# Down projection: the sums and low parts of the Strassen groups on VectorE instead of VectorE and GpSimd in turns

## The chip, the cores and the metric

The kernel runs on one core of a Trainium2 chip. The metric is the device time of one execution in microseconds (us). TensorE does the matmuls, VectorE (DVE in the rows) and GpSimd (POOL) the elementwise sums, ScalarE (ACT) the roundings and activations, and SyncE (SP) issues the loads and stores of this part.

## The reference

A layer with gated token mixers (windowed attention and an SSD scan), a cross-attention and a squared-ReLU MLP, in fp32, for 1024 tokens of width 1024. The part that matters here is the last one, the down projection of the MLP, a product of (1024 x 4096) by (4096 x 1024), and the final norm:

```python
        h = rmsnorm(x, norm_ffn[i])
        x = x + jnp.square(jax.nn.relu(h @ w_up[i])) @ w_down[i]
    return rmsnorm(x, norm_final)
```

## The kernel before, in words

An fp32 product is done as three matmuls of a reduced format: each operand is split into a high part (ScalarE rounds it, line 1305) and a low part (operand minus high part, line 1306), and high x high, high x low and low x high are accumulated.

`down_phase` walks over the 4096 hidden rows. The first 512 and the last 512 rows of the product are done plainly (`mm3`, lines 81 to 86). The 3072 rows between are three groups of 1024, each an object of class `Pair`: one level of Strassen-Winograd, so a group is seven products of 512-size blocks instead of eight. A product is 48 matmuls (line 1427): 4 row tiles t, and for each 4 slices k of the inner dimension by 3 matmuls. I call the seven products of a group its steps 1 to 7; `Pair.ORDER` gives their Strassen numbers (1, 2, 6, 5, 7, 3, 4).

While TensorE does one step, the other engines prepare the next one. A step's preparation is `split(n)`: 8 half tiles of 128 x 512 (4 of the left operand, 4 of the right), each one rounded by ScalarE and then subtracted (the low part). Some operands are sums of blocks; `early`, `s2`, `t6`, `s4` and `t4` make them with `op` (line 1271), also 128 x 512 each, 32 for a group, in place in the loaded rows or in the tiles `xy`. After every row tile VectorE adds the bank of PSUM to the running result (`add`, line 1331), since GpSimd does not read PSUM here.

The split tiles `kt` have four buffers, two for a step, so the rounding for the step after next can only start when TensorE is done with the step before. Rows of the hidden activations (`d_u`) and of the weights (`in_wdn_dram`) come in by SyncE (`load`, line 1255) into buffers that are reused as soon as their last reader is done.

TensorE's order is the written one; the other engines' queues are ordered by a scheduler from the code's dependencies and the units that `deal` hands out between the row tiles.

Of the kernel before, what the change touches and what calls it, by code (L numbers as in the profile page):

```python
# [7 lines left out]
F32 = mybir.dt.float32  # L8
# [3 lines left out]
ALU = mybir.AluOpType  # L12
# [57 lines left out]
def wload(kx, src, n=1024, hi=None, lo=None, eng=None):  # L70
    if hi is None:
        hi = kx.wp.tile([P, 1024], F32R, tag="wop", bufs=6, name="whi")[:, :n]
        lo = kx.wp.tile([P, 1024], F32R, tag="wop", bufs=6, name="wlo")[:, :n]
    split_in(kx, src, hi, lo, eng)
    return hi, lo
# [508 lines left out]
def attn_phase(kx, ins, dr):  # L584
    nc, tc = kx.nc, kx.tc
    V, A, G, PE = nc.vector, nc.scalar, nc.gpsimd, nc.tensor
    with tc.tile_pool(name="p2", bufs=1) as ap:
# [31 lines left out]
        for kv in range(4):  # L619
# [63 lines left out]
            def values(qb, t4):  # L683
                kb0, kb1 = max(qb - 1, 0), min(qb + 2, NT)
                nb = kb1 - kb0
                pts = []
                for kb in range(nb):
                    pt = kx.pp.tile([P, 512], F32, tag="p", name="pt")
                    for i in range(4):
                        PE.transpose(pt[:, i * P:(i + 1) * P], t4[:, i, kb * P:(kb + 1) * P], kx.ident)  # L690
                    ph = ap.tile([P, 512], F32R, tag="ph", bufs=4, name="ph")
                    pl = ap.tile([P, 512], F32R, tag="pl", bufs=4, name="pl")
                    A.activation(ph, pt, AF.Copy)
                    V.tensor_tensor(pl, pt, ph.bitcast(F32), ALU.subtract)
                    pts.append((ph, pl))
                op = kx.pp.tile([P, 512], F32, tag="p", name="op")
                for kb in range(nb):
                    v2 = vhl[:, kb0 + kb, kv].rearrange("p s q -> p (s q)")
                    PE.matmul(op, v2, pts[kb][0], start=kb == 0, stop=False)
                    PE.matmul(op, v2, pts[kb][1], start=False, stop=kb == nb - 1)  # L700
                oa = ap.tile([64, 512], F32, tag="oa", bufs=2, name="oa")
                ob = ap.tile([64, 512], F32, tag="ob", bufs=1, name="ob")
                A.activation(oa, op[0:64], AF.Copy)
                A.activation(ob, op[64:128], AF.Copy)
                G.tensor_tensor(oa, oa, ob, ALU.add)
                half = kv % 2
                nc.sync.dma_start(dr.at[kv // 2][qb // 4][64 * half:64 * half + 64, :, (qb % 4) * P:(qb % 4) * P + P],
                                  oa.rearrange("p (i c) -> p i c", i=4))
# [10 lines left out]
def merge_cross_phase(kx, ins, dr, x1_open):  # L719
    nc, tc = kx.nc, kx.tc  # L720
    V, A, G, PE = nc.vector, nc.scalar, nc.gpsimd, nc.tensor
    with tc.tile_pool(name="p3", bufs=1) as mp:
# [52 lines left out]
        def load_wo(ch, eng):  # L775
            ts = []
            for k2 in range(4):
                raw = kx.wp.tile([P, 1024], F32, tag="raw", bufs=kx.raw_bufs, name="raw")
                nc.sync.dma_start(raw, ins["wo"][ch, k2])
                for j in range(2):  # L780
                    t = t4k("wo")
                    rj = raw[:, j * 512:(j + 1) * 512]
                    A.activation(t[:, 0], rj, AF.Copy)
                    eng.tensor_tensor(t[:, 1], rj, t[:, 0].bitcast(F32), ALU.subtract)
                    ts.append(t)
            return ts
# [80 lines left out]
        def values(hd, p2, ok):  # L867
            ph, pl = p2
            op = kx.pp.tile([P, 512], F32, tag="p", name="xop")
            for kb in range(2):  # L870
                vs = slice(kb * 512 + hd * P, kb * 512 + hd * P + P)
                ks = slice(kb * 512, (kb + 1) * 512)
                mm3(kx, op, (vxh[:, vs], vxl[:, vs]), (ph[:, ks], pl[:, ks]), kb == 0, kb == 1)
            A.activation(ok[:, hd, 0], op, AF.Copy)
            V.tensor_tensor(ok[:, hd, 1], op, ok[:, hd, 0].bitcast(F32), ALU.subtract)
# [124 lines left out]
def kt_tile(kx):  # L1000
    return kx.mp.tile([P, 4, 2, 512], F32R, tag="kt", bufs=4, name="kt")
# [25 lines left out]
def split_wd(kx, ins, hl, m, raw, eng):  # L1027
    nc = kx.nc
    if ins is not None:
        nc.sync.dma_start(raw, ins["wdn"][m])  # L1030
    nc.scalar.activation(hl[0], raw, AF.Copy)
    eng.tensor_tensor(hl[1], raw, hl[0].bitcast(F32), ALU.subtract)


class Up:
# [138 lines left out]
    def quad(self, b, stage, nxt):  # L1174
# [21 lines left out]
        else:  # L1196
# [8 lines left out]
            after()  # L1205
        c12 = self.t2("c12")
        product(pb, 6, early)
        whole(c12, pb)
        after()
# [30 lines left out]
class Pair:  # L1240
# [26 lines left out]
        k, h = (int(name[1]) - 1, int(name[2]) - 1) if name[0] == "b" else (int(name[2]) - 1, int(name[1]) - 1)  # L1267
        return t[4 * k + j][:, 512 * h:512 * h + 512]

    def op(self, eng, out, x, y, alu, j):  # L1270
        eng.tensor_tensor(self.half(out, j), self.half(x, j), self.half(y, j), alu)

    def early(self, j):

        V, G, op = self.kx.nc.vector, self.kx.nc.gpsimd, self.op
        pool = self.fp if j < 2 else self.kx.wp
        self.xy[j] = pool.tile([P, D], F32, tag="raw", bufs=2, name="xy")
        return [lambda: op(V, "x", "a11", "a21", ALU.subtract, j), lambda: op(G, "y", "b22", "b12", ALU.subtract, j),
                lambda: op(V, "a21", "a21", "a22", ALU.add, j), lambda: op(G, "b12", "b12", "b11", ALU.subtract, j)]

    def eng(self, j, odd):
        return self.kx.nc.gpsimd if j % 2 != odd else self.kx.nc.vector

    def s2(self, j):
        self.op(self.eng(j, 0), "a11", "a21", "a11", ALU.subtract, j)

    def t6(self, j):
        self.op(self.eng(j, 1), "b11", "b22", "b12", ALU.subtract, j)

    def s4(self, j):  # L1290
        self.op(self.eng(j, 0), "a12", "a12", "a11", ALU.subtract, j)

    def t4(self, j):
        self.op(self.eng(j, 1), "b21", "b21", "b11", ALU.subtract, j)

    def split(self, n):

        nc = self.kx.nc
        left, right = {1: ("a11", "b11"), 2: ("a12", "b21"), 6: ("a11", "b11"), 5: ("a21", "b12"), 7: ("x", "y"),
                       3: ("a12", "b22"), 4: ("a22", "b21")}[n]  # L1300
        self.lr = lt, rt = kt_tile(self.kx), kt_tile(self.kx)

        def step(t, name, eng, j):
            src = self.half(name, j)
            nc.scalar.activation(t[:, j, 0], src, AF.Copy)  # L1305
            eng.tensor_tensor(t[:, j, 1], src, t[:, j, 0].bitcast(F32), ALU.subtract)  # L1306

        return [lambda t=t, name=name, eng=eng, j=j: step(t, name, eng, j) for j in range(4)
                for t, name, eng in ((lt, left, nc.vector), (rt, right, nc.gpsimd))]


def down_phase(kx, ins, dr, first, out):
# [252 lines left out]
```

## Time and profile before

| what | us |
|---|---|
| median of 3 runs | 2473.14 (2465.56 to 2475.99) |
| the profiled execution | 2473.64 |
| its span | 2471.9 |
| TensorE busy in the span | 2371.6 |
| VectorE busy | 1456.7 |
| GpSimd busy | 1199.7 |
| ScalarE busy | 1107.9 |

The span is the time from the first to the last recorded instruction; what lies around it is 1.7 us. Busy times overlap. The down projection's groups lie between 2173.7 and 2420.5 us of the span.

### The profile page before, as it was taken

Reading aid. Unit: us, or ns where it says so; the run is one execution under the profiler, and the core shown is the slowest. Engines: PE = TensorE matmul, PEld = TensorE weight load, DVE = VectorE, ACT = ScalarE, POOL = GpSimd, SP = SyncE. Lnnn points to the kernel's source line nnn. Section 1 sums busy time; section 2 is a strip of 40 time slices with the busy share of each in tenths; the row PEclk is TensorE's granted clock in tenths of the full one; section 3 lists DMA queues with packets and bytes.
Section 4 is the critical chain, followed back from the end, with each engine's and each line's share of the span. In section 5 each row is a group of like instructions: output and inputs, shape, how many; then the busy total and the mean of one; then the engine's idle time right before and its main releaser. Section 6 shows DMA issues by size and latency. Waiting matters only on the chain.

```text
span 2471.9 us, 32466 instructions
## 1 busy us (share of the span) xinstructions
PE 2371.6 (96%) x12012; PEld 1965.7 (80%) x12012; DVE 1456.7 (59%) x2120; ACT 1107.9 (45%) x2310; POOL 1199.7 (49%) x1013
## 2 busy tenths in 40 slices
PE   7899999999999999999999999999998999999998
PEld 6687887878888787777777878888986887877777
DVE  5747566575765654465564242334676456689884
ACT  5436354463635545566774242224543333133332
POOL 4235436353452633344553444324486444488870
PEclk9999999999999999999999999999999999999999
DMA  6214223231322322111116363512243345712301
GB/s 227 78 60 128 60 94 102 68 121 56 116 69 86 112 65 80 50 41 56 43 52 221 128 213 128 204 43 77 91 164 116 109 134 175 285 68 85 111 26 69
DMA packets 154926, 260.46 MB, mean 105 GB/s; under 512 B 11792, under 2 KB 86672, under 8 KB 154768
## 3 DMA queue, kind: packets, MB, share of 16 engines
q1 hardware_dynamic: 83872, 219.58, 25.6%
q10 hardware_dynamic: 70896, 38.81, 5.5%
q8 instruction: 95, 1.56, 0.2%
q14 instruction: 63, 0.52, 0.1%
HBM read 210.90 MB, written 47.45 MB: 105 GB/s over the span
## 4 chain that ended last, share of the span: by engine, by line
PE 57%; DVE 13%; POOL 11%; ACT 8%; issue 6%; DMA 4%; ACTq 0%; POOLq 0%; SPq 0%; DVEq 0%
PE pb L1146 6%; PE dps L1427 5%; PE mps L86 3%; PE mps L85 3%; PE mps L81 3%; PE pc L1146 3%; PE zp L85 2%; PE zp L81 2%; PE zp L86 2%; POOL wlo L67 2%; PE st L462 2%; DVE cx L350 2%; POOL prev L477 2%; POOL kt L1306 1%; ACT whi L66 1%
## 5 line engine op out<-in xcount | busy, mean ns | idle before, releaser
L67 POOL TENSOR_TENSOR wlo<-raw,whi 128x1024 fp32r<-128x1024 f32 x142 | 350.1, 2467 | 596.2 <-ACT whi L66 556.7
L66 ACT ACTIVATE whi<-raw 128x1024 fp32r<-128x1024 f32 x144 | 152.0, 1055 | 254.6 <-PE mps L85 115.5
L1427 PE MATMUL dps<-kt 128*128 128x512 f32 x1008 | 234.1, 394 | 12.8 <-POOL kt L1306 12.7
L1427 PEld LDWEIGHTS dps<-kt 128*128 128x128 f32 x1008 | 190.8, 190 | 56.0 <-POOL kt L1306 16.2
L81 PE MATMUL cps<-kt,whi 128*128 128x512 f32 x512 | 217.5, 425 | 8.6 <-DVE cx L350 8.6
L86 PE MATMUL cps<-kt,wlo 128*128 128x512 f32 x512 | 201.5, 394 | 0.0
L85 PE MATMUL cps<-kt,whi 128*128 128x512 f32 x512 | 200.8, 392 | 0.0
L1305 ACT ACTIVATE kt<-row 128x512 fp32r<-128x512 f32 x144 | 77.2, 618 | 156.7 <-PE dps L1427 119.7
L1306 POOL TENSOR_TENSOR kt<-row,kt 128x512 fp32r<-128x512 f32 x72 | 117.5, 1653 | 22.8 <-ACT kt L1305 22.8
L1092 POOL TENSOR_TENSOR wop<-w,wop 128x512 fp32r<-128x512 f32 x64 | 86.1, 1347 | 84.8 <-ACT wop L1091 75.9
L81 PEld LDWEIGHTS cps<-kt,whi 128*128 128x128 f32 x512 | 97.3, 190 | 34.6 <-issue 16.0
L85 PEld LDWEIGHTS cps<-kt,whi 128*128 128x128 f32 x512 | 97.5, 190 | 26.2 <-issue 7.2
L86 PEld LDWEIGHTS cps<-kt,wlo 128*128 128x128 f32 x512 | 96.9, 189 | 20.9
L120 POOL TENSOR_TENSOR rr<-rv,mhalf 128x1 f32<-128x1 f32 (+1 forms) x50 | 38.6, 772 | 152.2 <-DVE rv L118 149.6
L680 POOL TENSOR_SCALAR t<-t,den 128x384 f32<-128x384 f32 (+1 forms) x128 | 69.1, 559 | 82.0 <-DVE den L678 65.9
L81 PE MATMUL gps<-kt,whi 128*128 128x512 f32 x256 | 108.8, 425 | 0.0
L496 ACT ACTIVATE ef<-rows,ebias 128x128 f32<-128x128 f32 x256 | 83.2, 390 | 53.3 <-PE cb L511 49.9
L86 PE MATMUL mps<-yk,wlo 128*128 128x512 f32 x256 | 100.9, 394 | 4.8 <-POOL wlo L67 4.8
L1146 PE MATMUL pb<-kt,wop 128*128 128x512 f32 x384 | 94.8, 396 | 9.5 <-ACT c L1200 9.1
L86 PE MATMUL gps<-kt,wlo 128*128 128x512 f32 x256 | 101.5, 396 | 0.0
L85 PE MATMUL mps<-yk,whi 128*128 128x512 f32 x256 | 100.7, 393 | 0.2 <-DVE yk L734 0.2
L85 PE MATMUL gps<-kt,whi 128*128 128x512 f32 x256 | 100.9, 394 | 0.0
(381 smaller groups left out, 6964.8 us busy)
## 6 DMA issues: line engine op xcount, KB each, us to landing
rows<-d_cs ACTq DMA_DIRECT2D x128, 256.0 KB, 3.7
raw<-in_wssd_dram SPq DMA_DIRECT2D x48, 512.0 KB, 3.3
raw<-in_wup_dram SPq DMA_DIRECT2D x40, 512.0 KB, 3.6
raw<-in_wsb_dram SPq DMA_DIRECT2D x32, 512.0 KB, 3.2
d_u<-c SPq DMA_DIRECT2D x64, 256.0 KB, 2.3
row<-in_wdn_dram SPq DMA_DIRECT2D x28, 512.0 KB, 6.3
row<-d_u SPq DMA_DIRECT2D x28, 512.0 KB, 7.0
x<-in_x_dram SPq DMA_DIRECT2D x16, 512.0 KB, 6.0
```

What stands on the lines that cost most here:

```text
L66: nc.scalar.activation(hi, raw, AF.Copy)
L67: (eng or nc.gpsimd).tensor_tensor(lo, raw, hi.bitcast(F32), ALU.subtract)
L81: i = mm(out, l[0], r[0], start=first, stop=False)
L85: mm(out, l[0], r[1], start=False, stop=False)
L86: mm(out, l[1], r[0], start=False, stop=last)
L496: A.activation(ef[:, h], rows[:, 0, h], AF.Exp, bias=kx.ebias[:, b, j, 0, o:o + 1])
L680: G.tensor_scalar(t4[:, i, :n], t4[:, i, :n], den[:, i:i + 1], 1.0, ALU.mult, ALU.mult)
L1092: self.kx.nc.gpsimd.tensor_tensor(t[:, 1], src, t[:, 0].bitcast(F32), ALU.subtract)
L1146: self.kx.nc.tensor.matmul(ps, w[:, i, ks], act[:, k, j], start=start and k == 0 and m == 0, stop=k == 3 and m == 2, skip_group_check=True)
L1305: nc.scalar.activation(t[:, j, 0], src, AF.Copy)
L1306: eng.tensor_tensor(t[:, j, 1], src, t[:, j, 0].bitcast(F32), ALU.subtract)
L1427: PE.matmul(ps[t], lt[:, k, x, ts], rt[:, k, y], start=n in (1, 2, 5) and k == 0 and m == 0, stop=k == 3 and m == 2, skip_group_check=True)
```

## The change

Every sum (`early`, `s2`, `t6`, `s4`, `t4`) and every low part of the groups (`split`) is issued on VectorE. Before, about half of them were on GpSimd: the right operands' low parts, the sums of the right operand in `early`, and by turns (`eng`) the others. Nothing is added or removed, and no load is moved in the code. The low parts of the last 512 weight rows (`split_wd`, line 1032) and a tiny power (line 120) stay on GpSimd.

```diff
-    def op(self, eng, out, x, y, alu, j):
-        eng.tensor_tensor(self.half(out, j), self.half(x, j), self.half(y, j), alu)
+    def op(self, out, x, y, alu, j):
+        self.kx.nc.vector.tensor_tensor(self.half(out, j), self.half(x, j), self.half(y, j), alu)
...
-        return [lambda: op(V, "x", "a11", "a21", ALU.subtract, j), lambda: op(G, "y", "b22", "b12", ALU.subtract, j),
-                lambda: op(V, "a21", "a21", "a22", ALU.add, j), lambda: op(G, "b12", "b12", "b11", ALU.subtract, j)]
-
-    def eng(self, j, odd):
-        return self.kx.nc.gpsimd if j % 2 != odd else self.kx.nc.vector
+        return [lambda: op("x", "a11", "a21", ALU.subtract, j), lambda: op("y", "b22", "b12", ALU.subtract, j),
+                lambda: op("a21", "a21", "a22", ALU.add, j), lambda: op("b12", "b12", "b11", ALU.subtract, j)]
 
     def s2(self, j):
-        self.op(self.eng(j, 0), "a11", "a21", "a11", ALU.subtract, j)
+        self.op("a11", "a21", "a11", ALU.subtract, j)
 
     def t6(self, j):
-        self.op(self.eng(j, 1), "b11", "b22", "b12", ALU.subtract, j)
+        self.op("b11", "b22", "b12", ALU.subtract, j)
...
-        def step(t, name, eng, j):
+        def step(t, name, j):
             src = self.half(name, j)
             nc.scalar.activation(t[:, j, 0], src, AF.Copy)
-            eng.tensor_tensor(t[:, j, 1], src, t[:, j, 0].bitcast(F32), ALU.subtract)
-
-        return [lambda t=t, name=name, eng=eng, j=j: step(t, name, eng, j) for j in range(4)
-                for t, name, eng in ((lt, left, nc.vector), (rt, right, nc.gpsimd))]
+            nc.vector.tensor_tensor(t[:, j, 1], src, t[:, j, 0].bitcast(F32), ALU.subtract)
+
+        return [lambda t=t, name=name, j=j: step(t, name, j) for j in range(4)
+                for t, name in ((lt, left), (rt, right))]
```

The first place is step 6 of the first group, where step 7's operands are split (tiles `kt_19463` left, `kt_19464` right) and the next group's rows (`row_19487`, `row_19489`, `row_19512`, `row_19514`) have just been asked for. VectorE's queue before:

```order
L1306 TENSOR_TENSOR kt_19463<-row_18768,kt_19463 128x512
L1306 TENSOR_TENSOR kt_19463<-row_18776,kt_19463 128x512
L1331 TENSOR_TENSOR xl_18756<-xl_18756,dps_19064 128x512
L1306 TENSOR_TENSOR kt_19463<-row_18784,kt_19463 128x512
L1306 TENSOR_TENSOR kt_19463<-row_18792,kt_19463 128x512
L1271 TENSOR_TENSOR row_19331<-row_19331,row_19487 128x512
L1331 TENSOR_TENSOR xl_18758<-xl_18758,dps_19065 128x512
L1271 TENSOR_TENSOR row_19353<-row_19353,row_19512 128x512
L1331 TENSOR_TENSOR xl_18760<-xl_18760,dps_19066 128x512
L1331 TENSOR_TENSOR xl_18762<-xl_18762,dps_19067 128x512
```

GpSimd's queue before, in the same step:

```order
L1306 TENSOR_TENSOR kt_19464<-row_18770,kt_19464 128x512
L1306 TENSOR_TENSOR kt_19464<-row_18778,kt_19464 128x512
L1306 TENSOR_TENSOR kt_19464<-row_18786,kt_19464 128x512
L1306 TENSOR_TENSOR kt_19464<-row_18794,kt_19464 128x512
L1271 TENSOR_TENSOR xy_19548<-row_19489,row_19333 128x512
L1271 TENSOR_TENSOR row_19333<-row_19333 128x512
L1271 TENSOR_TENSOR xy_19549<-row_19514,row_19355 128x512
L1271 TENSOR_TENSOR row_19355<-row_19355 128x512
```

VectorE's queue of the changed kernel from the step's seventh low part to its last add (lines shifted by 3):

```order
L1303 TENSOR_TENSOR kt_19463<-row_18792,kt_19463 128x512
L1328 TENSOR_TENSOR xl_18758<-xl_18758,dps_19065 128x512
L1303 TENSOR_TENSOR kt_19464<-row_18794,kt_19464 128x512
L1271 TENSOR_TENSOR xy_19548<-row_19489,row_19333 128x512
L1271 TENSOR_TENSOR row_19331<-row_19331,row_19487 128x512
L1271 TENSOR_TENSOR row_19333<-row_19333 128x512
L1328 TENSOR_TENSOR xl_18760<-xl_18760,dps_19066 128x512
L1271 TENSOR_TENSOR row_19353<-row_19353,row_19512 128x512
L1271 TENSOR_TENSOR xy_19549<-row_19514,row_19355 128x512
L1271 TENSOR_TENSOR row_19355<-row_19355 128x512
L1328 TENSOR_TENSOR xl_18762<-xl_18762,dps_19067 128x512
```

The step's 18 instructions stand in one queue: eight low parts with two adds between them, then the sums that wait for the newly loaded rows, with the last two adds behind those.

The second place is the beginning of the phase, where the plain part's adds (tiles `dps`, line 1331 before) give banks of PSUM back. VectorE before:

```order
L1331 TENSOR_TENSOR xl_18760<-xl_18760,dps_18852 128x512
L1331 TENSOR_TENSOR xl_18760<-xl_18760,dps_18866 128x512
L1271 TENSOR_TENSOR row_18772<-row_18772,row_18776 128x512
L1331 TENSOR_TENSOR xl_18762<-xl_18762,dps_18880 128x512
L1271 TENSOR_TENSOR xy_18918<-row_18780 128x512
L1331 TENSOR_TENSOR xl_18762<-xl_18762,dps_18894 128x512
```

The same stretch of VectorE's queue in the changed kernel:

```order
L1328 TENSOR_TENSOR xl_18760<-xl_18760,dps_18852 128x512
L1328 TENSOR_TENSOR xl_18760<-xl_18760,dps_18866 128x512
L1271 TENSOR_TENSOR xy_18917<-row_18778,row_18774 128x512
L1271 TENSOR_TENSOR row_18774<-row_18774 128x512
L1271 TENSOR_TENSOR row_18772<-row_18772,row_18776 128x512
L1328 TENSOR_TENSOR xl_18762<-xl_18762,dps_18880 128x512
L1271 TENSOR_TENSOR xy_18918<-row_18780 128x512
L1271 TENSOR_TENSOR xy_18918<-row_18786,row_18782 128x512
L1328 TENSOR_TENSOR xl_18762<-xl_18762,dps_18894 128x512
```

Three sums of weight rows (`row_18774`, `row_18778`, `row_18782`, `row_18786`) now stand ahead of the last two adds.

## Rows read from the trace of the kernel before

**Rows 1.** Busy time of each engine in the stretch of the groups: stretch, its length, and for each engine busy us and instructions; then TensorE's granted clock as a share of 2.4 GHz, and the share and rate of the DMA engines.

```profile
2173.70:2420.47 246.77, 233.96 (x1009) 190.94 (x1009) 219.84 (x214) 93.66 (x172) 196.68 (x120) 0.99 0.20 73
```

**Rows 2.** TensorE's instructions in order of time, from the plain part's first matmul to the last part's first one: start, length of the run, instruction and count; in brackets how long the engine sat idle before it and whom it waited for.

```profile
2130.18 0.39 PE L81 MATMUL dps<-kt 128*128 128x512 f32 x1
...
2173.72 46.42 PE L1427 MATMUL dps<-kt 128*128 128x512 f32 x202
2221.50 32.95 PE L1427 MATMUL dps<-kt 128*128 128x512 f32 x144 [1.36 <-POOL kt L1306]
2256.21 11.18 PE L1427 MATMUL dps<-kt 128*128 128x512 f32 x48 [1.76 <-POOL kt L1306]
2269.64 34.56 PE L1427 MATMUL dps<-kt 128*128 128x512 f32 x144 [2.25 <-POOL kt L1306]
2305.57 32.95 PE L1427 MATMUL dps<-kt 128*128 128x512 f32 x144 [1.36 <-POOL kt L1306]
2340.11 10.49 PE L1427 MATMUL dps<-kt 128*128 128x512 f32 x45 [1.59 <-POOL kt L1306]
2352.63 0.98 PE L1427 MATMUL dps<-kt 128*128 128x512 f32 x3 [2.03 <-POOL kt L1306]
2355.98 64.65 PE L1427 MATMUL dps<-kt 128*128 128x512 f32 x278 [2.38 <-POOL kt L1306]
2420.47 0.39 PE L81 MATMUL dps<-wd,kt 128*128 128x512 f32 x1
```

**Rows 3.** The same columns as rows 1, in two short stretches right behind one of those waits.

```profile
2269.64:2271.64 2.00, 2.00 (x6) 1.58 (x7) 2.00 (x3) 0.00 (x0) 2.00 (x2) 0.61 0.00 0
2271.64:2273.64 2.00, 2.00 (x7) 1.59 (x6) 2.00 (x4) 0.00 (x0) 2.00 (x2) 0.54 0.00 0
```

**Rows 4.** VectorE and GpSimd in order of time ahead of one of those waits (first VectorE, then GpSimd).

```profile
2250.31 3.48 DVE L1271 TENSOR_TENSOR row<-row 128x512 f32<-128x512 f32 x2
2253.71 0.67 DVE L1331 TENSOR_TENSOR x<-x,dps 128x512 f32<-128x512 f32 x1
...
2249.80 1.74 POOL L1271 TENSOR_TENSOR row<-row 128x512 f32<-128x512 f32 x1
2251.49 1.75 POOL L1306 TENSOR_TENSOR kt<-row,kt 128x512 fp32r<-128x512 f32 x1
...
2254.89 1.26 POOL L1306 TENSOR_TENSOR kt<-row,kt 128x512 fp32r<-128x512 f32 x1
```

**Rows 5.** VectorE in order of time at three places where GpSimd ran nothing: low parts of the last part's rows (line 1024), sums, and adds out of PSUM; the last row is GpSimd where VectorE ran nothing.

```profile
2410.46 2.50 DVE L1024 TENSOR_TENSOR kt<-row,kt 128x512 fp32r<-128x512 f32 x4
2161.78 1.28 DVE L1271 TENSOR_TENSOR row<-row 128x512 f32<-128x512 f32 x2
2172.90 4.86 DVE L1331 TENSOR_TENSOR x<-x,dps 128x512 f32<-128x512 f32 x8
2164.44 2.55 POOL L1306 TENSOR_TENSOR kt<-row,kt 128x512 fp32r<-128x512 f32 x2
```

**Rows 6.** Instructions by line and shape in the groups' stretch: count, busy us and mean ns of one, then idle time before them and what ended it.

```profile
L1306 DVE TENSOR_TENSOR kt<-row,kt 128x512 fp32r<-128x512 f32 x68 | 88.4, 1327 | 1.6 <-ACT kt L1305 1.6
L1271 DVE TENSOR_TENSOR row<-row 128x512 f32<-128x512 f32 x28 | 45.3, 1632 | 5.4 <-POOL kt L1306 4.2 <-DMA row<-d_u 1.0
L1331 DVE TENSOR_TENSOR xl<-xl,dps 128x512 f32<-128x512 f32 x48 | 31.8, 677 | 11.8 <-PE dps L1427 11.8
L1331 DVE TENSOR_TENSOR x<-x,dps 128x512 f32<-128x512 f32 x42 | 27.1, 676 | 2.4 <-PE dps L1427 2.4
L1306 DVE TENSOR_TENSOR kt<-xy,kt 128x512 fp32r<-128x512 f32 x12 | 16.9, 1437 | 4.0 <-ACT kt L1305 4.0
L1271 DVE TENSOR_TENSOR xy<-row 128x512 f32<-128x512 f32 x8 | 14.0, 1773 | 0.0
...
L1306 POOL TENSOR_TENSOR kt<-row,kt 128x512 fp32r<-128x512 f32 x68 | 111.9, 1667 | 22.8 <-ACT kt L1305 22.8
L1271 POOL TENSOR_TENSOR row<-row 128x512 f32<-128x512 f32 x28 | 44.3, 1582 | 3.0 <-DVE kt L1306 1.9
L1306 POOL TENSOR_TENSOR kt<-xy,kt 128x512 fp32r<-128x512 f32 x12 | 19.8, 1663 | 8.9 <-ACT kt L1305 4.5 <-DMA row<-in_wdn_dram 4.5
L1271 POOL TENSOR_TENSOR xy<-row 128x512 f32<-128x512 f32 x8 | 12.5, 1562 | 0.8 <-issue 0.3 <-DMA row<-in_wdn_dram 0.2
L1032 POOL TENSOR_TENSOR wd<-row,wd 128x1024 fp32r<-128x1024 f32 x4 | 10.0, 2509 | 2.0 <-ACT wd L1031 2.0
```

**Rows 7.** ScalarE's roundings around step 6 of the first group, in order of time.

```profile
2230.46 4.28 ACT L1305 ACTIVATE kt<-row 128x512 fp32r<-128x512 f32 x8 [8.28 <-PE dps L1427]
```

**Rows 8.** SyncE's first issue of a load in that step, of eight; the loads of the last stretch of the program by source, with size and median time from issue to landing; and the longest piece of a load in the chain that ended last: start and length.

```profile
2231.93 0.32 SPq L1255 DMA_DIRECT2D row<-d_u  x1
...
row<-in_wdn_dram SPq DMA_DIRECT2D x28, 512.0 KB, 6.3
row<-d_u SPq DMA_DIRECT2D x28, 512.0 KB, 7.0
...
2204.97 7.92 DMA row<-in_wdn_dram
```

**Rows 9.** GpSimd in order of time at the phase's beginning, where its sums wait for loads of weight rows.

```profile
2148.26 1.29 POOL L1271 TENSOR_TENSOR xy<-row 128x512 f32<-128x512 f32 x1 [7.86 <-DMA row<-in_wdn_dram]
2152.01 1.30 POOL L1271 TENSOR_TENSOR xy<-row 128x512 f32<-128x512 f32 x1 [0.65 <-DMA row<-in_wdn_dram]
```

More of the change, by code (lines that the diff above doesn't have):

```diff
@@ L1268, in half @@
         return t[4 * k + j][:, 512 * h:512 * h + 512]
-    def op(self, eng, out, x, y, alu, j):
-        eng.tensor_tensor(self.half(out, j), self.half(x, j), self.half(y, j), alu)
+    def op(self, out, x, y, alu, j):
+        self.kx.nc.vector.tensor_tensor(self.half(out, j), self.half(x, j), self.half(y, j), alu)
     def early(self, j):
-        V, G, op = self.kx.nc.vector, self.kx.nc.gpsimd, self.op
+        op = self.op
         pool = self.fp if j < 2 else self.kx.wp
         self.xy[j] = pool.tile([P, D], F32, tag="raw", bufs=2, name="xy")
-        return [lambda: op(V, "x", "a11", "a21", ALU.subtract, j), lambda: op(G, "y", "b22", "b12", ALU.subtract, j),
-                lambda: op(V, "a21", "a21", "a22", ALU.add, j), lambda: op(G, "b12", "b12", "b11", ALU.subtract, j)]
-    def eng(self, j, odd):
-        return self.kx.nc.gpsimd if j % 2 != odd else self.kx.nc.vector
+        return [lambda: op("x", "a11", "a21", ALU.subtract, j), lambda: op("y", "b22", "b12", ALU.subtract, j),
+                lambda: op("a21", "a21", "a22", ALU.add, j), lambda: op("b12", "b12", "b11", ALU.subtract, j)]
     def s2(self, j):
-        self.op(self.eng(j, 0), "a11", "a21", "a11", ALU.subtract, j)
+        self.op("a11", "a21", "a11", ALU.subtract, j)
     def t6(self, j):
-        self.op(self.eng(j, 1), "b11", "b22", "b12", ALU.subtract, j)
+        self.op("b11", "b22", "b12", ALU.subtract, j)
     def s4(self, j):
-        self.op(self.eng(j, 0), "a12", "a12", "a11", ALU.subtract, j)
+        self.op("a12", "a12", "a11", ALU.subtract, j)
     def t4(self, j):
-        self.op(self.eng(j, 1), "b21", "b21", "b11", ALU.subtract, j)
+        self.op("b21", "b21", "b11", ALU.subtract, j)
     def split(self, n):
```

## The prediction, made before the changed kernel was run

> **What bounds the kernel now.** I read the windows first. In the 246.77 us of the three groups TensorE is busy for nearly all, VectorE for 219.84 and GpSimd for 196.68 [rows 1]: three engines near their limit, so small differences between them show as waits. TensorE's own order in time says what is lost. From its first matmul of the groups at 2173.72 to the next part's first at 2420.47 are 246.75 us [rows 2]. The plain part before it, 192 matmuls without a wait, takes 2173.72 - 2130.18 = 43.54 us, 0.2268 us for one [rows 2]. The groups' 1008 matmuls would take 228.6 us at that pace. So 18.2 us are lost, and nothing in this change can give back more.
>
> The waits are all on GpSimd's low parts (line 1306), and they lie where a group ends and the next begins: the first run holds 202 matmuls, four steps of 48 and 10 of the fifth [rows 2]. The eleventh matmul of a step is the first that needs the low part of the right operand's last slice, so TensorE stood there and waited for the very last low part of that step. The other runs end in the same way (144 or 48 further on).
>
> A part of the 18.2 us is clock. Behind the wait that ends at 2269.64 the granted clock is 0.61 and 0.54 for 4 us [rows 3]: nearly all of it at 1.2 GHz, after TensorE had been idle for 2.25 us [rows 2]. The run of 144 matmuls there takes 34.56 us, and two others of 144 take 32.95; the last run, 278 matmuls, takes 64.65 where 0.39 + 277 x 0.2268 = 63.2 would do [rows 2]. That is 1.6 + 1.4 = 3.0 us. The other 15.2 us are the waits themselves.
>
> Why GpSimd is late shows where both engines work on 128 x 512 operands in SBUF. They advance in step, 1.7 us for each: VectorE's two sums take 3.48 us, GpSimd's beside them 1.74 and 1.75; VectorE's add out of PSUM between them takes 0.67 [rows 4]. Where GpSimd runs nothing, the same VectorE instructions come every 0.60 us: (2.50 - 0.69) / 3 for low parts, 1.28 - 0.68 for sums, and (4.86 - 0.68) / 7 for adds [rows 5]. GpSimd alone needs 1.25 [rows 5]. So one instruction on each engine costs 1.7 us together, about 0.60 + 1.25 less a little overlap: they take turns, and two on VectorE would cost 1.2.
>
> **The change, part by part.** *What moves.* Of the sums and low parts 68 + 28 + 12 + 8 = 116 are on each engine in this stretch, and 90 adds are on VectorE [rows 6]. All 322 on VectorE at 0.60 us are 193 us, 85% of the 228.6 that TensorE needs; before, VectorE was busy for 219.84 [rows 1]. VectorE gets more instructions and less busy time. The price of 0.60 is the one that I choose; its upper bound is the length of one instruction, 0.68 (as in 677 ns for an add [rows 6]), if none overlapped the next.
>
> *Whether each step fits.* By the changed program's queue the steps of the first two groups hold 18, 14, 12, 18, 16, 18, 18 and then 18, 16, 12, 18, 16, 18, 18 VectorE instructions; a step of TensorE is 48 x 0.2268 = 10.9 us. 18 x 0.60 = 10.8. Before, GpSimd had up to 8 in such a step: 8 x 1.7 = 13.6 us. What TensorE waits for are the eight low parts, and they stand first, with two adds between them. ScalarE's eight roundings begin some 0.3 us after the step before has left the buffers and take 4.28 us [rows 7]; so VectorE starts about 1.0 us into a step and ends the last low part at 1.0 + 10 x 0.60 = 7.0 us. It is due at the next step's eleventh matmul, 10.9 + 2.3 = 13.1 us (less the time of a semaphore). That is 6 us to spare in each step.
>
> *The adds.* They now queue behind sums. A bank is written again only two steps later, so an add may be late by several us at no cost; if that cover went, each us of delay would be one of TensorE's.
>
> *Sums behind loads.* In step 6 of the first two groups the sums of the next group's rows follow the low parts directly. The eight loads are asked for from 2231.93 on, about 1.8 us into the step (which began 38 matmuls behind 2221.50, at 2230.1), and land 6.3 to 7.0 us later in the median, at worst 7.9 [rows 2, 8]. In the changed queue the fourth of these loads can be issued when the fourth low part is done, 1.0 + 4 x 0.60 + 0.2 = 3.6 us into the step; it lands at 9.9 (11.5 at worst). VectorE comes to the first of the sums at 7.0, waits for the second load (2.4 + 6.3 = 8.7), runs six instructions and the two adds, and ends at about 13.5: the next step starts 2.6 us late on VectorE instead of 1.0. The steps of 18 keep that lateness and those of 16 and 12 take it back. The last low part is then done at 8.6 of 13.1. Price: nothing, with 4.5 us to spare; if that were gone, each further us would cost one at both group borders.
>
> *The phase's beginning.* Three sums of weight rows now stand ahead of two adds that free banks of PSUM. Their rows come at 2148.26 and 2152.01 [rows 9], so those adds end near 2151 and 2153.5, and TensorE wants the two banks again from 2130.18 + 96 x 0.2268 + 6 x 0.68 = 2156.0 on [rows 2]. Nothing, with 2.5 us to spare.
>
> *What stays on GpSimd.* Four low parts of 2.5 us [rows 6] fall into the third group, where the later steps hold 12 instructions (7.2 us of 10.9). 4 x 2.5 us of VectorE's waiting fits there.
>
> *Sum.* Of 18.2 us I keep what is lost at the borders of steps even without a wait: the runs of 144 take 32.95 where 0.39 + 143 x 0.2268 = 32.8 would do [rows 2], 0.13 us for three steps, 0.9 for 21. The gain is 17.3 us: 15.2 of waits and 3.0 of clock, less 0.9. The profiled execution took 2473.64, 0.5 above the median of 2473.14: 2473.64 - 17.3 = 2456.3, so 2456.
>
> **A page on the pace.** The eight adds of [rows 5] are 0.68 long and come every 0.60, so an instruction begins before the one ahead has ended. The Trainium skill, "VectorE: DVE Perf Modes", section "The DRAIN you can't avoid", says that the next instruction does not start until the pipe is empty, which speaks against this change; by it I would take the whole length as the pace, and the trace does not bear that out here. A second place of the Trainium skill, "Perfetto Trace Analysis", section "Optimizing Scalar/DVE Operations", lets GpSimd take work when VectorE is saturated but warns that the two share a port; the 1.7 us of [rows 4] are this case's figure for that warning.
>
> **The rivals.** *A slower VectorE.* With waits among its own results VectorE could need 0.69 us for each (0.68 and a start). A step of 18 is then 12.4 us against 10.9, and VectorE falls behind by 1.5 us in each; over steps 4 to 7 and the next 1 (18, 16, 18, 18, 18), with 1 us at the loads, the lateness grows to about 8 us, past the 6 that are spare. I get some 2.5 us of waits at the first border and 4.5 at the second: the gain is about 10, and the time 2463. For it: many sums read what the instruction before them wrote. Against: the pace in [rows 5].
>
> *Late rows stop VectorE* (the other side). One queue now holds low parts behind sums that wait for rows; with a landing time L the next step is L - 5.5 us late, and TensorE waits once that is over 7.1, so from L = 12.6 us on, at both borders. The gain is gone at L = 12.6 + 17.3 / 2 = 21.3 us, and with 24 us the time is 2456 + 2 x 11.4 = 2479. Against: 7.9 is the longest load of the chain [rows 8].
>
> *It doesn't do what it says*: VectorE is slow for another reason than GpSimd's turns. Then 232 instructions at their present 1.4 us and 90 adds at 0.6 are 379 us, 150 more than TensorE's: 2606. Against it are the rows in which the very same forms run at 0.60 alone.
>
> *Half the waits return elsewhere* (ScalarE's roundings, loads earlier or later than now): 2473.64 - 9 = 2465.
>
> **How the numbers follow.** Chances: the forecast 0.70, with 2451 to 2461 for itself; slower VectorE 0.16; late rows 0.05; not the port 0.03; half elsewhere 0.06. The three runs of before lie within -0.3% and +0.1% of their median, so the range is wider than the sum alone: 2449 to 2468 takes in the forecast, the slower VectorE and half elsewhere. A measurement of this kernel tells about 0.5% from no change, 12.4 us; the forecast is 0.7% faster. So faster 0.72 (nearly all of the forecast and a quarter of the slower VectorE), same 0.22, slower 0.06.
>
> **What would show it right or wrong.** Right: TensorE's 1008 matmuls in one run of about 229.5 us without a wait over 1 us, granted clock 1.00 throughout; VectorE's low parts and sums near 0.69 in the mean, and its busy time in the groups falling below 205 us. Wrong: low parts of 1 us and more with GpSimd idle (not the port), TensorE waiting for VectorE's low parts at steps 1 and 2 of a group (pace), or VectorE's sums waiting many us for rows in step 6 (loads). If the runs without waits were not slower in their clock for those waits, 3 us of the gain would be missing.

## The result and the profile after

The changed kernel takes 2455.07 us (median of 4 runs, 2452.77 to 2457.70), the kernel before on the same chip 2474.05 (4 runs, 2465.56 to 2475.99). The ratio is 0.9928, with a 95% interval of 0.9913 to 0.9942. The forecast was 2456.0. The profiled execution took 2457.36 us, with a span of 2455.6.

The page's busy times and its row for the groups' matmuls:

```profile
PE 2369.6 (96%) x12012; PEld 1964.5 (80%) x12012; DVE 1446.1 (59%) x2252; ACT 1107.8 (45%) x2310; POOL 991.5 (40%) x881
...
L1424 PE MATMUL dps<-kt 128*128 128x512 f32 x1008 | 228.6, 389 | 0.0
```

TensorE in order of time from the groups' first matmul to the last part's first one:

```profile
2175.71 228.64 PE L1424 MATMUL dps<-kt 128*128 128x512 f32 x1008
2404.19 0.39 PE L81 MATMUL dps<-wd,kt 128*128 128x512 f32 x1
```

Where [rows 2] showed eight runs with seven waits on GpSimd between them, there is one run of 1008 matmuls and no wait. The groups take 2404.19 - 2175.71 = 228.48 us instead of 246.75: 18.27 us gained.

The same stretch by engine, with the columns of [rows 1]:

```profile
2175.70:2404.20 228.50, 228.50 (x1010) 189.20 (x1009) 202.59 (x325) 93.70 (x172) 11.16 (x4) 1.00 0.21 79
```

VectorE runs 325 instructions here instead of 214 and is busy for 202.59 us instead of 219.84: half as many instructions again, and 17 us less busy time. GpSimd falls from 196.68 us to 11.16. The clock is 1.00 throughout.

VectorE by line and shape in that stretch, then GpSimd, with the columns of [rows 6]:

```profile
L1303 DVE TENSOR_TENSOR kt<-row,kt 128x512 fp32r<-128x512 f32 x136 | 87.5, 695 | 0.0
L1271 DVE TENSOR_TENSOR row<-row 128x512 f32<-128x512 f32 x56 | 37.5, 711 | 0.1
L1328 DVE TENSOR_TENSOR xl<-xl,dps 128x512 f32<-128x512 f32 x48 | 32.6, 680 | 14.0 <-PE dps L1424 13.8
L1303 DVE TENSOR_TENSOR kt<-xy,kt 128x512 fp32r<-128x512 f32 x24 | 17.0, 757 | 1.5 <-ACT kt L1302 1.5
L1271 DVE TENSOR_TENSOR xy<-row 128x512 f32<-128x512 f32 x16 | 10.6, 683 | 1.2 <-DMA row<-in_wdn_dram 1.2
...
L1032 POOL TENSOR_TENSOR wd<-row,wd 128x1024 fp32r<-128x1024 f32 x4 | 11.2, 2800 | 228.1 <-ACT wd L1031 228.1
```

The low parts that took 1327 and 1437 ns in the mean in [rows 6] take 695 and 757, the sums 711 and 683 instead of 1632 and 1773. The adds out of PSUM are as long as they were (680 ns after, 677 before). VectorE idles about as long as before (228.50 - 202.59 = 25.9 us, against 26.9 in [rows 1]): it does more in less busy time because each of these instructions is shorter.

The whole time moved by a little less than the groups in the profiled pair (2473.64 - 2457.36 = 16.28, where the medians differ by 19.0) because this execution reached the groups 2.0 us later (2175.71 against 2173.72). The part ahead of the groups scatters: over eleven profiled executions of kernels with the same code up to the down projection, the groups begin between 2168.44 and 2177.24. So below I give the length of the groups beside each median. Where TensorE never waits it repeats exactly, 228.48 us in all six such executions; with waits it does not (233.84 and 230.06 us for one and the same kernel below), and each length, the 246.75 of the kernel before included, comes from one execution.

### The profile page after: what moved, and what is told of

Its sections match the earlier page's. It is cut to its first block, busy times and chain, and to the rows that moved or that the text cites. A ratio compares the mean times of both kernels' runs of the same rounds, so it can differ in the third digit from the quotient of the medians.

```text
span 2455.6 us, 32420 instructions
## 1 busy us (share of the span) xinstructions
PE 2369.6 (96%) x12012; PEld 1964.5 (80%) x12012; DVE 1446.1 (59%) x2252; ACT 1107.8 (45%) x2310; POOL 991.5 (40%) x881
## 4 chain that ended last, share of the span: by engine, by line
PE 64%; DVE 12%; POOL 8%; ACT 7%; issue 5%; DMA 3%; ACTq 0%; POOLq 0%; SPq 0%; DVEq 0%
PE dps L1424 9%; PE pb L1146 6%; PE mps L81 3%; PE mps L86 3%; PE mps L85 3%; PE pc L1146 3%; PE zp L85 2%; PE zp L81 2%; PE zp L86 2%; PE st L462 2%; POOL wlo L67 2%; DVE cx L350 2%; POOL prev L477 2%; POOL cb_t L476 1%; PE wops L81 1%
## 5 line engine op out<-in xcount | busy, mean ns | idle before, releaser
L1424 PE MATMUL dps<-kt 128*128 128x512 f32 x1008 | 228.6, 389 | 0.0
L1032 POOL TENSOR_TENSOR wd<-row,wd 128x1024 fp32r<-128x1024 f32 x4 | 11.2, 2800 | 228.1 <-ACT wd L1031 228.1
```

The lines of the kernel that those rows point to most:

```text
L1424: PE.matmul(ps[t], lt[:, k, x, ts], rt[:, k, y], start=n in (1, 2, 5) and k == 0 and m == 0, stop=k == 3 and m == 2, skip_group_check=True)
```

## The experiments

The forecast rests on the two engines taking turns, so that work on GpSimd was no help. The main rivals: only the choice of who makes which operand counts, since TensorE waited for GpSimd's low parts alone; and VectorE's pace is nearer 0.69, hidden by slack. Each edit is against the changed kernel unless said otherwise; each ratio is to the kernel before, run on the same chip.

**Half of the change.** Sums on VectorE, the right operands' low parts back on GpSimd:

```diff
-            nc.vector.tensor_tensor(t[:, j, 1], src, t[:, j, 0].bitcast(F32), ALU.subtract)
+            eng = nc.vector if t is lt else nc.gpsimd
+            eng.tensor_tensor(t[:, j, 1], src, t[:, j, 0].bitcast(F32), ALU.subtract)
```

> All sums on VectorE as in the change, but the right operands' low parts back on GpSimd (four in a step). If VectorE and GpSimd take turns (1.7 us for one instruction on each, as in the rows of before): a step of 18 costs VectorE 14 x 0.6 + 4 x 1.1 = 12.8 us against TensorE's 10.9, so it falls behind by some 1.9 us in each of them, and TensorE waits again for low parts at the group borders, less than before: about 2464 us (2457 to 2468), VectorE's low parts near 1.3 us in the mean. If only GpSimd's own length of work was the trouble (8 instructions of 1.25 us in a crowded step), its four leave it idle half the time and nothing waits: 2455 us.

Measured: 2464.34 us (2460.67 to 2465.88), ratio 0.9956 (0.9940 to 0.9971); the groups take 237.06 us. TensorE's waits in the groups (whom it waited for, us in total, times, longest), and the means of VectorE's and GpSimd's low parts and of VectorE's sums by line:

```profile
PE dps L1425 <- DVE kt L1304: 6.4, 7, 1.3
```

```profile
L1304 DVE TENSOR_TENSOR kt<-row,kt 128x512 fp32r<-128x512 f32 x68 | 76.4, 1154 | 0.3 <-ACT kt L1302 0.3
L1271 DVE TENSOR_TENSOR row<-row 128x512 f32<-128x512 f32 x56 | 58.0, 1059 | 3.2 <-DMA row<-d_u 2.9
...
L1304 POOL TENSOR_TENSOR kt<-row,kt 128x512 fp32r<-128x512 f32 x68 | 108.3, 1623 | 77.4 <-ACT kt L1302 77.4
```

As expected by turns, and it says more: GpSimd now idles 77.4 us ahead of its low parts and TensorE waits for it nowhere, yet TensorE waits, for *VectorE's* low parts, which are 1154 ns long. So GpSimd's work makes VectorE late as well. In the kernel before, GpSimd was truly the last: at the seven waits of [rows 2] VectorE had finished the left operand's low parts 2.8 to 6.2 us before GpSimd finished the right operand's. Ahead of the wait that ends at 2256.21, in the kernel before, VectorE's last two low parts, then GpSimd (the two rows between, a sum at 2249.80 and a low part at 2251.49, are in [rows 4]):

```profile
2247.50 2.88 DVE L1306 TENSOR_TENSOR kt<-row,kt 128x512 fp32r<-128x512 f32 x2
...
2248.10 1.74 POOL L1306 TENSOR_TENSOR kt<-row,kt 128x512 fp32r<-128x512 f32 x1
...
2253.32 1.61 POOL L1271 TENSOR_TENSOR row<-row 128x512 f32<-128x512 f32 x1
2254.89 1.26 POOL L1306 TENSOR_TENSOR kt<-row,kt 128x512 fp32r<-128x512 f32 x1
```

VectorE's end at 2250.38, GpSimd's at 2256.15. GpSimd's low parts and sums alternate here, while the changed kernel's one queue has all low parts of a step ahead of its sums. So the change also altered the order. How much of the gain GpSimd's low parts ahead of its sums would have brought by themselves was not run, and this half does not settle it, since it gives VectorE all the sums.

The other half, low parts on VectorE and sums divided as before (edit against the kernel before):

```diff
-                for t, name, eng in ((lt, left, nc.vector), (rt, right, nc.gpsimd))]
+                for t, name, eng in ((lt, left, nc.vector), (rt, right, nc.vector))]
```

> All low parts on VectorE, the sums divided between VectorE and GpSimd as before (about three on GpSimd in a step of 18). By turns: 15 x 0.6 + 3 x 1.1 = 12.3 us in such a step, 1.4 us late in each, which the 6 us to spare nearly cover: about 2458 us (2455 to 2463). By GpSimd's length of work alone: 2455 us. If the gain came from the sums alone: near 2474 us.

Measured: 2455.07 us (2451.62 to 2458.64), ratio 0.9920 (0.9904 to 0.9937), the same median as the whole change. But the groups took 233.84 us, 5.4 more than the changed kernel's; that execution reached them early, at 2168.44. So it was run once more beside the changed kernel.

> The low parts alone on VectorE, the sums divided as before: a second look with more runs, beside the changed kernel itself (the next run). In its first profile the three groups took some 234 us, 5.5 more than the 228.5 of the changed kernel, with two waits of TensorE in the third group, but its median was that of the changed kernel, 2455.1, since the program had reached the groups 7 us earlier in that execution. If the sums on GpSimd still cost what the groups show, the median is 4 to 7 us above that of the changed kernel, and the groups take 232 to 236 us again. If the low parts carry the whole gain, the two medians agree within 2 us.

> The changed kernel once more, as the other side of the comparison with the low parts alone: 2455, the groups 228.5 us.

Measured: 2458.78 us (2453.90 to 2461.50, 6 runs), ratio 0.9939 (0.9923 to 0.9954), against 2455.60 (2449.47 to 2458.89, 6 runs), ratio 0.9923 (0.9907 to 0.9939), for the changed kernel. The groups took 230.06 us and 228.48. TensorE's waits in the groups, in the first and in the second execution of the low parts alone:

```profile
PE dps L1427 <- DVE kt L1306: 3.1, 2, 2.0
```

```profile
PE dps L1427 <- DVE kt L1306: 1.1, 1, 1.1
```

The two medians differ by 3.2 us, between what the two answers wanted, and their intervals overlap; the groups' 230.06 us are less than the 232 to 236 expected if the sums still cost. The traces say that sums on GpSimd cost the groups 1.6 to 5.4 us; the times can't tell that from nothing. The low parts carry 12.9 to 16.7 of the 18.3 us. The sums alone (the first half) gave 246.75 - 237.06 = 9.7, so the halves add up to more than the whole, as they can where a wait appears only past a point.

**Is it the turns?** The changed kernel, with GpSimd repeating the right operands' low parts into a tile that nobody reads (the lines that make the tile are left out here and below):

```diff
...
+            if t is rt:
+                nc.gpsimd.tensor_tensor(self.scr, src, t[:, j, 0].bitcast(F32), ALU.subtract)
```

> The changed kernel, and beside it GpSimd repeats the right operands' low parts (four in a step, two operands in SBUF) into a tile that nobody reads. By turns: each of them holds VectorE up by about 1.1 us, so a step of 16.6 instructions in the mean costs 10.0 + 4.4 = 14.4 us against 10.9; over the fourteen steps of the first two groups 49 us less 6 to spare, and a few in the third: about 2500 us (2485 to 2515), VectorE's instructions again at 1.2 to 1.8 us. If GpSimd disturbs nobody and only its results were late: 2455 us.

Measured: 2507.29 us (2505.99 to 2508.85), ratio 1.0133 (1.0117 to 1.0150); the groups take 279.06 us. The waits in the groups and the stretch by engine:

```profile
PE dps L1428 <- DVE kt L1304: 30.4, 22, 2.7
```

```profile
2173.76:2452.82 279.06, 248.63 (x1010) 197.10 (x1010) 275.65 (x330) 94.09 (x172) 142.56 (x84) 0.94 0.18 65
```

One step of it in order of time, VectorE and then GpSimd:

```profile
2214.97 4.69 DVE L1304 TENSOR_TENSOR kt<-xy,kt 128x512 fp32r<-128x512 f32 x4
...
2215.60 6.91 POOL L1306 TENSOR_TENSOR scr<-xy,kt 128x512 f32<-128x512 f32 x4 [11.75 <-ACT kt L1303]
```

Nothing that VectorE or TensorE does has changed, no instruction or load waits for GpSimd's copies, and the time rises by 52 us. The groups are 50.6 us longer: 30.4 are waits for VectorE's low parts, and 20.1 are TensorE's own busy time (248.63 against 228.50), with the granted clock at 0.94 in the mean. Four low parts on VectorE take 4.69 us beside GpSimd's copies, where four alone take 2.50; GpSimd's four take 6.91, 1.7 each. VectorE is busy for 275.65 of 279.06 us: it has become the bound. The rival that only the choice of who makes an operand counts falls.

**What kind of access?** The same places, but GpSimd only writes: it fills the right low part with zeros before VectorE writes it.

```diff
+            if t is rt:
+                nc.gpsimd.memset(t[:, j, 1].bitcast(F32), 0.0)
```

> The changed kernel, with GpSimd filling the right operands' low-part tiles with zeros (four in a step, no operand read) ahead of VectorE's writing them. If every access of GpSimd to SBUF takes a turn, VectorE loses the length of each fill: with 0.5 us some 2 us in a step, 12 against 10.9, about 2464 us. If the turns are taken only between instructions that read two operands in SBUF and a GpSimd instruction that reads SBUF, VectorE keeps its 0.60 us: 2455 to 2458 us.

Measured: 2453.00 us (2451.33 to 2454.86), ratio 0.9912 (0.9897 to 0.9927); the groups take 228.48 us, as without it. TensorE, VectorE and GpSimd at one step:

```profile
2173.08 228.64 PE L1426 MATMUL dps<-kt 128*128 128x512 f32 x1008
...
2206.59 2.50 DVE L1305 TENSOR_TENSOR kt<-xy,kt 128x512 fp32r<-128x512 f32 x4
...
2205.94 1.94 POOL L1304 MEMSET kt<- 128x512 f32 x4 [8.94 <-PE dps L1426]
```

The four zero fills run to 2207.88, and the four low parts that began at 2206.59 take 2.50 us as ever. Over the whole of the groups VectorE is busy for 202.90 us, against 202.59 without the fills. So GpSimd's writes into SBUF cost VectorE nothing here; its instructions that read two operands there do. The Trainium skill, "SBUF — State Buffer", section "Who interferes with whom", says just that: a VectorE instruction with two SBUF inputs contends with a GpSimd instruction that reads SBUF, not with one that only writes it. These two runs agree with it.

**The pace of VectorE.** The right low parts are repeated on VectorE, four extra instructions in each step, or two (the second with `if t is rt and j % 2`):

```diff
...
+            if t is rt:
+                nc.vector.tensor_tensor(self.scr, src, t[:, j, 0].bitcast(F32), ALU.subtract)
```

> The changed kernel, with VectorE itself repeating the right operands' low parts (four more instructions in each step, 84 in all) into a tile that nobody reads; GpSimd stays idle. At 0.60 us for each a step of the first two groups costs 20.6 x 0.60 = 12.4 us against 10.9: 1.5 x 14 = 21 us less the 6 to spare, and the third group catches nothing up on TensorE: about 2470 us (2463 to 2476). At 0.69 us for each: 14.2 us a step, 46 less 6: about 2495 us. If VectorE has much more room than the counts say: 2455 us.

> The same with two more VectorE instructions in each step (42 in all). At 0.60 us: 18.6 x 0.60 = 11.2 us against 10.9, 0.3 x 14 = 4 us behind at most, which the 6 us to spare cover: 2455 to 2457 us, no wait on TensorE. At 0.69 us: 12.8 us, 27 less 6: about 2476 us.

Measured: 2488.11 us (2485.24 to 2492.50, 6 runs), ratio 1.0060 (1.0042 to 1.0078), with four; 2460.93 (2458.69 to 2468.57, 9 runs), ratio 0.9956 (0.9940 to 0.9971), with two. Both lie above what I expected at 0.60 and below what 0.69 would give. The groups take 260.92 and 238.04 us. With four extras, the waits in the groups; then a stretch in which VectorE never idles (its columns: length, VectorE's busy time and instructions, granted clock, DMA share and rate) and the whole of the groups:

```profile
PE dps L1428 <- DVE kt L1304: 18.3, 14, 2.6
PE dps L1428 <- ACT kt L1303: 2.7, 2, 1.3
```

```profile
2203.52:2282.30 78.78, 78.78 (x133) 0.96 0.29 100
...
2175.41:2436.33 260.92, 239.94 (x1010) 192.61 (x1008) 253.36 (x407) 95.33 (x172) 12.18 (x4) 0.96 0.20 69
```

In 78.78 us lie 131 whole instructions (the row counts one at each end that only touches it): 0.60 us each. So the pace was right, and under full load, with low parts, sums, adds and repeats mixed. What I had left out is in the second row. 322 + 84 = 406 instructions at 0.60 are 244 us, but VectorE is busy for 253.36. Most of these 9 us are turns again: GpSimd's four instructions of line 1032 lengthen four pairs of low parts from 1.28 us to 2.90, 3.16, 3.44 and 3.22, 7.6 us in all. The rest to 260.92 is VectorE's own idle time, another 7.6 us, most of it (5.7) waiting for roundings and for TensorE's results. And of TensorE's 260.92 - 228.48 = 32.4 us only 21.0 are waits; 11.4 are its own busy time, grown with the granted clock at 0.96 in the mean of the groups.

With two extras all the waits are in the third group. TensorE there, and VectorE and GpSimd at one of the four instructions:

```profile
2336.24 10.97 PE L1428 MATMUL dps<-kt 128*128 128x512 f32 x47 [0.90 <-DVE kt L1304]
2348.03 0.50 PE L1428 MATMUL dps<-kt 128*128 128x512 f32 x1 [0.82 <-ACT kt L1303]
...
2372.54 1.31 PE L1428 MATMUL dps<-kt 128*128 128x512 f32 x3 [1.79 <-DVE kt L1304]
2374.94 32.97 PE L1428 MATMUL dps<-kt 128*128 128x512 f32 x134 [1.09 <-DVE kt L1304]
...
2354.63 3.16 DVE L1304 TENSOR_TENSOR kt<-row,kt 128x512 fp32r<-128x512 f32 x2
...
2354.25 2.40 POOL L1032 TENSOR_TENSOR wd<-row,wd 128x1024 fp32r<-128x1024 f32 x1 [33.05 <-DVE row L1272]
```

A pair of low parts takes 3.16 us beside a GpSimd instruction of 2.40, where it takes 1.28 alone. Three of the four instructions hold up a pair of low parts in this way; the first, earlier in the group, holds up a pair of sums (2.89 us). If that makes the waits, moving those four to VectorE as well must remove them, though VectorE then has more to do:

```diff
-                    split_wd(kx, None, hl, j, fraw[j], G)
+                    split_wd(kx, None, hl, j, fraw[j], V)
```

> The kernel with two extra VectorE instructions in each step, and the third group's four remaining low parts (wd, 128 x 1024) moved from GpSimd to VectorE. With two extras alone the time was 2460.9, 5.9 us above the changed kernel, and all of TensorE's waits (5.1 us, 6 of them) lay in the third group, where each of these four GpSimd instructions holds up a pair of VectorE's low parts: 3.16 to 3.25 us instead of 1.28. If these turns made the waits: VectorE has in the third group 104 instructions at 0.60 and four of about 1.3 us, 68 us of 76, the waits are gone, and the time is 2455 to 2457. If the lateness that the extras build up in the first two groups makes them (28 steps' worth of extras, 232 + 28 = 260 instructions at 0.60 against 152 us): the waits stay, and the time is 2460 or more.

(The 28 there are extra instructions, two in each of the 14 steps of the first two groups.)

Measured: 2456.42 us (2453.22 to 2460.10), ratio 0.9941 (0.9923 to 0.9959); the groups take 230.10 us. What is left of the waits, and the four instructions on VectorE (their shortest, median and longest in ns):

```profile
PE dps L1428 <- ACT kt L1303: 0.8, 1, 0.8
PE dps L1428 <- DVE kt L1304: 0.2, 1, 0.2
```

```profile
L1032 DVE TENSOR_TENSOR wd<-row,wd x4: 1217/1218/1221, 2378.2 to 2397.2; 128x1024 fp32r<-128x1024 f32 x4
```

The waits fall from 5.1 us to 1.0, with VectorE at 225.36 us of work in 230.10. So the turns were the cause of 4.1 us, as far as one execution of each can say. The 1.0 us is at the same matmuls as in the run with two extras alone; that it comes from the extras' lateness is likely, not shown.

**The same edit elsewhere.** The up projection ahead of this part has the same low parts on GpSimd (112 instructions, 1.35 to 1.50 us each), and TensorE waits there for 9.3 us in one place. First those low parts on VectorE, then also four sums' low parts of the same class (`put("s1", f1, G)` to `put("s4", f4, G)`, with `V` for `G`):

```diff
-        self.kx.nc.gpsimd.tensor_tensor(t[:, 1], src, t[:, 0].bitcast(F32), ALU.subtract)
+        self.kx.nc.vector.tensor_tensor(t[:, 1], src, t[:, 0].bitcast(F32), ALU.subtract)
```

> The changed kernel, and the same change in the up projection ahead of it: the 64-odd low parts of its weights (line 1092) on VectorE. In that stretch (1800 to 2129 us) TensorE loses about 12 us, most of it in one wait of 9.3 us behind ScalarE near 1840 us. If that wait is the end of a chain through GpSimd's low parts: some us to 10 us faster than the changed kernel, 2445 to 2452. If the chain is held by loads and roundings: 2455, the same.

> As the run before, and the low parts of the up projection's four summed operands on VectorE as well (16 more of 128 x 512). If the turns of the two engines make the wait near 1840 us: 2440 to 2450. If VectorE, which is busy for 32 of 40 us there, becomes the late one: 2458 to 2465.

Measured: 2443.69 us (2440.72 to 2451.50), ratio 0.9877 (0.9848 to 0.9906), and 2441.20 (2439.56 to 2447.40), ratio 0.9876 (0.9850 to 0.9901). Both beat the changed kernel by 11 to 14 us. The stretch of that wait by engine, in the changed kernel:

```profile
1840.00:1870.00 30.00, 20.70 (x87) 16.74 (x86) 22.08 (x24) 11.78 (x23) 23.17 (x16) 0.83 0.43 141
```

The same in the second of these kernels, with the four sums' low parts on VectorE too, then TensorE's run of the groups there:

```profile
1840.00:1870.00 30.00, 30.00 (x133) 24.57 (x132) 25.36 (x41) 13.27 (x25) 0.00 (x0) 1.00 0.40 144
```

```profile
2157.73 228.64 PE L1424 MATMUL dps<-kt 128*128 128x512 f32 x1008
```

In this stretch TensorE's 9.3 us of idle and the clock of 0.83 are gone: 133 matmuls in 30 us instead of 87. VectorE runs 41 instructions there instead of 24 for 3 us more of busy time. TensorE's wait by name, in the changed kernel, in the first of these kernels and, as the largest that is left in the part, in the second:

```profile
PE pb L1146 <- ACT c L1200: 9.3, 1, 9.3
...
PE pb L1146 <- ACT c L1200: 3.8, 1, 3.8
...
PE pb L1146 <- DVE rv L118: 2.2, 1, 2.2
```

So with the 112 low parts alone the wait shrinks to 3.8 us, and with the 16 others it is gone, while a wait of 2.2 us for VectorE, not there before, stands 23 us ahead of the stretch. That turns made this wait too is argued from the same edit's effect; which step of the chain was late was not tested. In the second kernel the groups begin at 2157.73, 11 to 20 us earlier than in the eleven executions above, and take the same 228.48 us. The first kernel's profiled execution, its slowest, reached them at 2169.82, within the spread of those eleven, so that run's trace shows the shorter wait but not the gain of its median.

Last, this version with the four instructions of line 1032 on VectorE too:

> The fastest version so far (2441.2: the up projection's low parts and four of its sums on VectorE too) with the third group's four remaining low parts (wd) moved to VectorE as well. In the changed kernel TensorE waited nowhere in the groups, so these four cost nothing there: 2441, within 2 us. If they cost something that the waits don't show, such as later adds in the last part, 2436 to 2439.

Measured: 2439.01 us (2438.15 to 2446.98), ratio 0.9873 (0.9853 to 0.9893); the groups 228.48 us. No difference that can be told: with VectorE at its normal load those turns are covered.

## Why the prediction was right, step by step

**The sum.** 18.2 us were to be had in the groups and 17.3 forecast; 18.27 came. The 0.9 us kept for the borders of steps was wrong: 1008 matmuls take 228.48 us, 0.2267 each, so the borders cost nothing. The 0.13 us more in the runs of 144 [rows 2] belonged to the start behind a wait: the run of 3 there has it too (0.98 us, where 0.39 + 2 x 0.2267 = 0.84 would do). The division of the 18.2 was off as well: TensorE idled for 246.77 - 233.96 = 12.8 us [rows 1], not 15.2, and its own busy time fell by 5.5 us (233.96 to 228.50), of which the forecast named 3.0, as clock. The total escaped this because the 15.2 was a remainder. Two of the seven waits, those behind 202 and 538 matmuls, also lie in the fifth step of a group and not where one ends. The clock came back with the waits, as forecast: 1.00 in the whole stretch, against 0.99 in [rows 1]. That the median came within 1 us of the forecast is partly luck: executions of one kernel differ by 5 to 10 us, and the medians by 19.0 where the groups gave 18.27.

**The pace.** 0.60 was right for a VectorE that works without a break, as the run with four extras shows. The mean length of an instruction, 680 to 757 ns, is not the pace. Busy time in the groups is 202.59 us, below the 205 named as the mark, and 9 above 322 x 0.60 = 193: turns with line 1032 are a part of it (four low parts of 4.28 us instead of 2.50, shown below, where what stays on GpSimd is discussed); the starts after a pause may be the rest.

**Fit of a step.** VectorE's rows in order of time: the third step's first low parts and the last; the first of the sums in step 6 of the first group; the eight low parts of step 7; and the last low part of the second group's first step.

```profile
2198.34 2.50 DVE L1303 TENSOR_TENSOR kt<-row,kt 128x512 fp32r<-128x512 f32 x4
...
2203.76 0.69 DVE L1303 TENSOR_TENSOR kt<-row,kt 128x512 fp32r<-128x512 f32 x1
...
2238.32 0.69 DVE L1271 TENSOR_TENSOR xy<-row 128x512 f32<-128x512 f32 x1 [1.25 <-DMA row<-in_wdn_dram]
...
2243.26 2.49 DVE L1303 TENSOR_TENSOR kt<-row,kt 128x512 fp32r<-128x512 f32 x4
...
2246.27 2.49 DVE L1303 TENSOR_TENSOR kt<-row,kt 128x512 fp32r<-128x512 f32 x4
...
2259.49 0.69 DVE L1303 TENSOR_TENSOR kt<-row,kt 128x512 fp32r<-128x512 f32 x1
```

Step 3 begins at 2175.71 + 2 x 10.88 = 2197.47; its first low part starts 0.9 us into it (1.0 forecast) and its last ends at 2204.45, 7.0 us in (7.0 forecast).

**Sums behind loads.** Step 6 begins at 2230.1. The first sum waits 1.25 us for its load and starts 8.2 us in (8.7 forecast); step 7's low parts start 2.3 us into their step (2.6 forecast) and end at 2248.76, 7.8 us in, where 8.6 was forecast and 13.1 allowed. The lateness goes on into the second group, as forecast: its first step begins at 2175.71 + 7 x 10.88 = 2251.87, and its last low part ends at 2260.18, 8.3 us in, the latest in the first two groups. At the second border no sum waits for a load. So the wait that the forecast feared is there, in size and place, and its cover holds.

**The beginning.** The two adds end at 2152.90 and 2155.25 in an execution that is 2.0 us later, so 2150.9 and 2153.3 against the 2151 and 2153.5 forecast:

```profile
2152.22 0.68 DVE L1328 TENSOR_TENSOR xl<-xl,dps 128x512 f32<-128x512 f32 x1
...
2154.57 0.68 DVE L1328 TENSOR_TENSOR xl<-xl,dps 128x512 f32<-128x512 f32 x1
```

**What stays on GpSimd.** Priced at nothing, and nothing it cost. But the four instructions are 2.8 us long in the mean, not 2.5, and they use up cover. Four low parts of the third group's fourth step, the last of that step, and the GpSimd instruction beside the four:

```profile
2363.11 4.28 DVE L1303 TENSOR_TENSOR kt<-xy,kt 128x512 fp32r<-128x512 f32 x4 [1.55 <-ACT kt L1302]
...
2370.32 0.67 DVE L1303 TENSOR_TENSOR kt<-xy,kt 128x512 fp32r<-128x512 f32 x1
...
2362.63 2.40 POOL L1032 TENSOR_TENSOR wd<-row,wd 128x1024 fp32r<-128x1024 f32 x1 [1.70 <-ACT wd L1031]
```

That step begins at 2175.71 + 17 x 10.88 = 2360.67, and its low parts end at 2370.99, 10.3 us in: the latest of all, with 2.8 us left of the 6 forecast for each step. The two extras show that this cover ends soon: with them the term cost 4 us.

**The rivals.** A slower VectorE falls by the pace. Late rows fall: the one wait is 1.25 us. That it doesn't do what it says falls by the lengths of the low parts. One rival was not on the list: the order of low parts and sums in GpSimd's queue, which the change altered along with the engine; its share of the gain is open, while the run with GpSimd's copies shows what the turns alone can cost. The page of the Trainium skill that was taken to speak against the change ("VectorE: DVE Perf Modes", section "The DRAIN you can't avoid") would, by the sentence that the prediction took from it, have made the pace 0.68; the trace under full load shows 0.60 again. The same paragraph adds that a next instruction that is not held starts earlier. With this the trace agrees (0.60 us from start to start, 0.68 long), so the section read whole did not speak against the change.

**Where I was wrong.** In expectations behind the prediction: 2470 with four extras and 2455 to 2457 with two. I counted VectorE's instructions at their pace, but not the turns with line 1032 or VectorE's idle time once TensorE is late as well, which TensorE's lower clock behind its waits draws out. Those were 18 of the 33 us by which four extras lengthen the run, and most of the 6 with two.

## What to carry to other kernels

Before giving GpSimd half of an elementwise load, read what the pair costs: here two instructions on VectorE take 1.2 us, and one on each engine 1.7, so that the helper made both late: with its sums taken away, TensorE waited for VectorE instead. Look too at the order in the helper's queue, which this change altered without testing it. And look for the same pattern in the stretches where another wait is named: the same one-line edit in the up projection was worth 11 us more. When a margin is tested by adding work, count what the late engine holds up in return, the clock among it, not the added instructions alone.

## What the runs showed of the hardware

- GpSimd's zero fills into SBUF (0.48 us each for 128 x 512, four in 1.94 us) do not delay VectorE's two-input instructions (four in 2.50 us), while GpSimd's two-input instructions nearly double their time: 4.69 us for four.
- VectorE's adds with one operand in PSUM keep their 0.68 us whatever GpSimd runs in these kernels (674 to 682 ns in the mean).
- A longer GpSimd instruction holds VectorE up for longer: a pair of low parts takes 3.16 us beside one of 2.40, and 1.28 alone. The 128 x 1024 low part that GpSimd makes in those 2.40 us takes 1.22 us on VectorE.
- GpSimd is held up too: where VectorE already ran its instructions one behind the other, the first GpSimd instruction of that form was recorded with 4.54 us (two extras) and 5.02 us (four) instead of 2.40.
